# Pinning the order of three engines in the recurrent stage of a hybrid decoder layer

## The chip, the cores and the metric

The kernel runs on one core of one Trainium2 chip. The metric is the device time of one execution in microseconds (us). Of the engines, TensorE (PE; its weight loads are PEld), VectorE (DVE), ScalarE (ACT) and GpSimd (POOL) compute, and SyncE (SP) issues most DMAs. Each takes its instructions in the order in which they stand in its own program; semaphores tie the engines to each other.

## The reference

One decoder layer, batch 1, 1024 tokens, width 1024, all in float32. After an RMSNorm one input projection makes the columns of two branches; both branches are gated by a SiLU, joined, projected out, added to x and normed again.

```
p = rms_norm(x) @ w_in                      # 1024 x 8320
p_tm = p_tm + (prev_token(p_tm) - p_tm) * mu_shift
# RWKV-7, 16 heads of 64, one step per token:
sa    = state @ (-kk)
state = state * decay + sa (kk*a)^T + v k^T
y     = state @ r       # then group norm, + bonus (r.k.r_k) v, * silu(gate)
# 16 heads of attention over three dilated windows, * silu(gate)
out = rms_norm(x + concat(y_rwkv, y_att) @ w_out)
```

## The kernel before

Every big product is made exact enough by splitting each operand into a high and a low float32r part: three matmuls of 128x128 by 128x512 for each 128 rows of the sum, so 24 matmuls for one half-job, that is 128 columns of the projection for 512 tokens (`proj_steps`, L174).

The recurrent stage (`rwkv`, from L284) works on 16 units: eight pairs of heads by two halves of the sequence. A unit's 512 tokens are eight chunks of 64. Its work is a pipeline over four turns of one loop over p: in the turn of unit p, unit p+2 is prepared (`prepare`, `products`: decays, their running sums and exponentials, norms, the products inside a chunk), unit p+1 is turned and its triangular systems are inverted (`late`, `invert`), unit p runs the recurrence (`chain`), and unit p-1 is normed, gated and stored (`finish`).

A turn is cut into 24 slots, three for each chunk. `chain` gives one piece for each slot: first (L707's helper `spread` copies z to zd), second (ud), third (Sd, the new state). Each piece is a small matmul, then a copy of one half on VectorE (L704, L707) and, after it, of the other half on ScalarE (L705, L708), whose result the next piece's matmul reads. The other steps are lists of (slot, function); the loop appends them to the slot's list `ev[s]` and calls them in that order: chain, finish, late, invert, prepare and products. After each slot `advance(4)` issues four matmuls of the projection stream.

The stream (`stream`, L182) works through the projection's columns. At the start of a job, `wload` (L161) issues the two DMAs for the next job's weights, their casts on ScalarE (L170) and their remainders (L171; on VectorE for this stage's columns). After the 24th matmul of a half-job the bank is emptied at once (`take`): for most columns the token shift, L213 on ScalarE and L216 on VectorE. Two PSUM banks serve the stream; one bank (tag `tr`) serves the transposes, the bonus and the inversion in turn, and two (pa0, pa1) serve the decay, the products and the turning of the output.

The program is written with a scheduling layer that sees all instructions. What stands above is only the order of emission: within the data's dependences the layer chooses the order of each engine itself, from emission order as priority and an estimated time for each instruction. It also places all semaphores, and it lets only one engine at a time work on a PSUM bank.

After this stage, attention runs with the rest of the projection stream between its own matmuls, and then the output projection.

Of the kernel before, what the change touches and what calls it, by code (L numbers as in the profile page):

```python
# [19 lines left out]
KT = DM // 128  # L20
# [10 lines left out]
NSLOT = 3 * NC_  # L31
AHEAD = 120
OFILL = 8
WARM = (1, 0)
V_AT = (-2, 3, -1)
COLS = (2, 2, 2, 4, 5, 6, 6, 6, 7, 8, 8, 8, 9, 9, 10)
DECAY = float(np.exp(-0.5))
# [8 lines left out]
class Kern:  # L46
# [114 lines left out]
    def wload(self, src, wp, eng):  # L161

        nc = self.nc
        wl = wp.tile([128, KT, 128], F32R, name="wl")
        wh = wp.tile([128, KT, 128], F32R, name="wh")
        for i in range(2):
            raw = wp.tile([128, KT // 2, 128], F32, name="wraw")
            ks = slice(4 * i, 4 * i + 4)
            nc.sync.dma_start(out=raw, in_=src[i * 512:(i + 1) * 512].rearrange("(kt p) c -> p kt c", p=128))
            nc.scalar.copy(out=wh[:, ks], in_=raw)  # L170
            eng.tensor_tensor(out=wl[:, ks], in0=raw, in1=wh[:, ks].bitcast(F32), op=ALU.subtract)  # L171
        return wh, wl

    def proj_steps(self, w, h, q):  # L174
        wh, wl = w
# [6 lines left out]
    def stream(self, jobs):  # L182

        load = lambda job: self.wload(self.t["w_in"][:, job[0]:job[0] + 128], self.wp,
                                      self.nc.vector if job[0] < ATT0 else self.nc.gpsimd)
        w = load(jobs[0])
        for i, (_, halves, take) in enumerate(jobs):
            wn = load(jobs[i + 1]) if i + 1 < len(jobs) else None
            for h in halves:
                q = self.ps_proj.tile([128, HALF], F32, name="pq", tag="proj")  # L190
                steps = self.proj_steps(w, h, q)
                for m in steps[:-1]:
                    m()
                    yield
                steps[-1]()
                take(h, q)
                yield
            w = wn

    def advance(self, n):  # L200
# [83 lines left out]
    def rwkv(self, pairs=range(NPAIR), apairs=range(NPAIR)):  # L284
        nc = self.nc
        with ExitStack() as ctx:
# [37 lines left out]
            units = [dict(h=h, pr=pr) for pr in pairs for h in range(2)]  # L324
            for i, d in enumerate(units):
                d["AR"], d["Vd"] = self.ARs[i % 3], self.Vds[i % 2]
            N = len(units)
            self.flow = self.stream(self.jobs(units, apairs))
            next(self.flow)
            self.taken = 1  # L330
# [4 lines left out]
            self.lora_w(units[0])  # L335
            for p in range(-2, N):
# [3 lines left out]
                if dC:  # L340
                    put(enumerate(self.chain(dC, get(p + 1) if dC["h"] == 0 else None)))
                if dF:
                    put(self.finish(dF))
                if dI:
                    put(self.late(dI))
                    put(self.invert(dI, self.Us[(p + 1) % 2]))
                if dA:
                    lag = WARM[p + 2] if p < 0 else 0
                    put([(n + lag, f) for n, f in self.prepare(dA) + self.products(dA)])
                if get(p + 3) and get(p + 3)["h"] == 0:  # L350
                    ev[12].append(lambda d=get(p + 3): self.lora_w(d))
                elif get(p + 3):
                    get(p + 3)["lw"] = get(p + 2)["lw"]
                if p == -2:
                    px = self.prep_x(1, self.lng, tags, ba)
                    for s in range(4):
                        ev[s].append(lambda: [next(px, None) for _ in range(2)])
                    ev[4].append(lambda: [None for _ in px])
                n = 5 if p < 0 else 2 if dA is not None and get(p + 3) is None else 4
                for s in range(NSLOT):  # L360
                    for f in ev[s]:
                        f()
                    self.advance(n)
            for _, f in self.finish(units[-1]):
                f()

# [3 lines left out]
    def lora_w(self, d):  # L370

        nc = self.nc
        pc = slice(d["pr"] * 128, d["pr"] * 128 + 128)
        raw = self.mid.tile([128, 128], F32, name="lraw", bufs=1)
        nc.sync.dma_start(out=raw[0:64], in_=self.t["w_up"][:, pc])
        nc.sync.dma_start(out=raw[64:128], in_=self.t["a_up"][:, pc])
        hi = [self.mid.tile([128, 128], F32R, name=f"lhi{i}", bufs=1) for i in range(2)]
        lo = self.llo
        for i in range(2):
            a, b = slice(64 * i, 64 * i + 64), slice(64 - 64 * i, 128 - 64 * i)  # L380
            nc.scalar.copy(out=hi[i][a], in_=raw[a])
            nc.scalar.copy(out=hi[i][b], in_=raw[a])
            nc.gpsimd.tensor_tensor(out=lo[i][a], in0=raw[a], in1=hi[i][a].bitcast(F32), op=ALU.subtract)
        d["lw"] = hi, lo

    def prepare(self, d):

        nc = self.nc
        V, S, G = nc.vector, nc.scalar, nc.gpsimd
        h, pr = d["h"], d["pr"]  # L390
# [48 lines left out]
        t = {}  # L439
# [13 lines left out]
        def norm():  # L453
            sqt = t["q"]
            nq = self.mid.tile([128, 4, 2], F32, name="nq")
            V.tensor_reduce(out=nq, in_=sqt, axis=AX.X, op=ALU.add)
            rn = d["rn"] = self.mid.tile([128, NC_], F32, name="rn", bufs=3)
            for par in range(2):
                for e in range(2):
                    V.tensor_scalar(out=rn[e * 64:e * 64 + 64, par::2], in0=nq[par * 64:par * 64 + 64, :, e], scalar1=1e-24,  # L460
                                    scalar2=-2.0, op0=ALU.max, op1=ALU.mult)
            V.reciprocal(out=rn, in_=rn)
            d["rn1"] = self.mid.tile([64, NC_], F32, name="rn1", bufs=3)
            S.copy(out=d["rn1"], in_=rn[64:128])

        def removal():
            ks, ta, W, Ux = d["ks"], d["ta"], d["W"], d["Ux"]
# [17 lines left out]
        def bonus_parts():  # L485
            rs = d["rs"]
            V.scalar_tensor_tensor(out=rs, in0=rs, scalar=self.hrk[:, pr:pr + 1], in1=d["ks"], op0=ALU.mult, op1=ALU.mult)
            bh, bl = d["bs"] = [self.tmp(t, n, dt=F32R) for t, n in (("kr3", "bh"), ("vr3", "bl"))]
            S.copy(out=bh, in_=rs)
            G.tensor_tensor(out=bl, in0=rs, in1=bh.bitcast(F32), op=ALU.subtract)  # L490
        return [(2, square), (4, squares), (5, norm), (7, decay), (8, rates), (9, logs), (10, lambda: sums(0)), (11, lambda: sums(1)),
                (11, growth), (12, decrease), (13, removal), (14, removal2), (15, removal3), (16, receptance), (21, bonus_parts)]

    def late(self, d):

# [94 lines left out]
    def invert(self, d, U):  # L590

        nc = self.nc
        V, S, G = nc.vector, nc.scalar, nc.gpsimd
# [3 lines left out]
        rs = lambda g: slice(32 * g, 32 * g + 32)  # L597
        t = {}
# [57 lines left out]
        lo = [slice(e * 64, e * 64 + 32) for e in range(2)]  # L656
        hi = [slice(e * 64 + 32, e * 64 + 64) for e in range(2)]
# [19 lines left out]
        def m4c():  # L677
# [122 lines left out]
    def attention(self, ctx, pairs=range(NPAIR), filler=None):  # L800
# [44 lines left out]
        for j, (pr, e) in enumerate(heads):  # L845
# [6 lines left out]
            for i, (qb, n) in enumerate(tiles):  # L852
# [311 lines left out]
```

## Time and profile before

| what | value |
|---|---|
| time, median of 3 runs | 1554.56 us (1554.13 to 1555.15) |
| the profiled execution | 1555.3 us, its span 1553.6 us |
| TensorE busy | 1486.1 us, 96% of the span |
| VectorE busy | 1009.3 us, 65% |
| ScalarE busy | 897.6 us, 58% |
| GpSimd busy | 442.0 us, 28% |
| recurrent units | from about 114 us to 843 us of the span |

Busy time of an engine is the union of its instructions' spans. Matmuls overlap in the pipeline, so a matmul that lasts 0.4 us may start 0.23 us after the one before it; TensorE's busy share says little about how close it is to its limit. The granted clock is given as a share of the full 2.4 GHz.

### The profile page before, as it was taken

What the parts mean: (1) busy time and instruction counts of PE and PEld (TensorE: products, weight loads), DVE (VectorE), ACT (ScalarE), POOL (GpSimd) and SP (SyncE); (2) the same over time, 40 slices, a digit from 0 to 9 for tenths busy, and PEclk for the clock granted to TensorE, in tenths of its full rate; (3) what the DMA queues carried; (4) which work ended last, traced back from release to release, by engine and by line L of the source; (5) the groups of instructions that cost most, each with busy time, mean ns of one, the idle gap of its engine ahead of it and who ended that gap; (6) DMA issues with size and microseconds to landing.
All of it is one profiled execution on the core that took longest, in us unless ns stands there. A gap on an engine that the chain in (4) does not pass through costs nothing.

```text
span 1553.6 us, 29135 instructions
## 1 busy us (share of the span) xinstructions
PE 1486.1 (96%) x10721; PEld 1201.3 (77%) x10721; DVE 1009.3 (65%) x2776; ACT 897.6 (58%) x2080; POOL 442.0 (28%) x563
## 2 busy tenths in 40 slices
PE   5999999999999999999999999999999999899997
PEld 4877777777777777777777788888888888787886
DVE  6866776667776677766743557667676666956144
ACT  6655666666676666666643556555565565655221
POOL 3211111111111121112211534334443343456442
PEclk9999999999999999999999999999999999999999
DMA  6321111111111111111111201111111111426452
GB/s 199 90 48 33 41 40 39 41 34 40 47 32 41 47 33 41 39 38 41 34 39 34 70 28 42 35 35 34 38 52 34 36 55 55 159 92 203 142 161 99
DMA packets 178829, 94.87 MB, mean 61 GB/s; under 512 B 58413, under 2 KB 164606, under 8 KB 178686
## 3 DMA queue, kind: packets, MB, share of 16 engines
q1 hardware_dynamic: 174942, 86.19, 19.4%
q10 hardware_dynamic: 3744, 6.82, 1.3%
q8 instruction: 84, 1.38, 0.4%
q14 instruction: 59, 0.48, 0.1%
HBM read 75.01 MB, written 17.83 MB: 60 GB/s over the span
## 4 chain that ended last, share of the span: by engine, by line
PE 60%; DVE 17%; ACT 16%; issue 3%; DMA 2%; POOL 1%; SPq 0%; DVEq 0%; ACTq 0%; POOLq 0%
PE pq L179 28%; PE oq L1048 10%; PE o L994 3%; PE z L693 3%; PE T L693 3%; PE mp L921 2%; PE sp L954 2%; ACT Y L745 1%; DVE I L422 1%; ACT MV L569 1%; PE sp L974 1%; ACT Vd L513 1%; DVE TB L604 1%; ACT shtmp L213 1%; PE pa L559 1%
## 5 line engine op out<-in xcount | busy, mean ns | idle before, releaser
L179 PE MATMUL pq<-xh,wh 128*128 128x512 f32 x1040 | 429.1, 413 | 0.0
L179 PE MATMUL pq<-xl,wh 128*128 128x512 f32 x1040 | 412.3, 396 | 0.0
L179 PE MATMUL pq<-xh,wl 128*128 128x512 f32 x1040 | 303.3, 409 | 0.0
L179 PEld LDWEIGHTS pq<-xh,wh 128*128 128x128 f32 x1040 | 195.9, 188 | 32.6 <-ACT xh L157 0.3
L179 PEld LDWEIGHTS pq<-xl,wh 128*128 128x128 f32 x1040 | 196.4, 189 | 30.9 <-DVE xl L158 0.4
L179 PEld LDWEIGHTS pq<-xh,wl 128*128 128x128 f32 x1040 | 184.5, 189 | 31.9
L1048 PE MATMUL oq<-ow,qr 128*128 128x512 f32 x512 | 161.9, 394 | 1.2 <-ACT ow L1029 0.6
L982 POOL TENSOR_TENSOR pl<-p,ph 128x512 fp32r<-128x512 f32 (+2 forms) x96 | 102.3, 1072 | 202.2 <-ACT ph L981 182.4
L923 DVE CUSTOM_DVE_ANT_0 mp<-mp,maskq 128x512 f32<-128x512 f32 (+1 forms) x192 | 105.5, 570 | 68.4 <-PE mp L921 59.9
L977 ACT ACTIVATE p<-p 128x512 f32<-128x512 f32 (+2 forms) x144 | 64.6, 452 | 104.2 <-DVE p L976 103.3
L171 POOL TENSOR_TENSOR wl<-wraw,wh 128x512 fp32r<-128x512 f32 x64 | 85.5, 1354 | 110.4 <-PE pq L179 58.4
L1043 POOL TENSOR_TENSOR vr<-kr,qr 128x512 fp32r<-128x512 f32 (+2 forms) x68 | 90.8, 1340 | 80.5 <-ACT qr L1042 70.0
L1048 PEld LDWEIGHTS oq<-ow,qr 128*128 128x128 f32 x512 | 95.9, 188 | 22.8 <-ACT ow L1029 1.1
L1048 PE MATMUL oq<-ow,vr 128*128 128x512 f32 x256 | 101.2, 395 | 1.9 <-POOL vr L1043 1.9
L170 ACT CAST wh<-wraw 128x512 fp32r<-128x512 f32 x138 | 80.7, 616 | 28.6 <-PE pq L179 23.4
L1042 ACT CAST qr<-kr 128x512 fp32r<-128x512 f32 (+2 forms) x68 | 40.2, 594 | 93.5 <-PE oq L1048 52.0
L976 DVE TENSOR_TENSOR p<-sp,maskt 128x512 f32<-128x512 f32 (+2 forms) x144 | 65.2, 457 | 43.3 <-PE sp L974 41.9
L570 POOL TENSOR_SCALAR_AFFINE_SELECT MV<-MV 64x512 f32<-64x512 f32 x64 | 47.8, 747 | 125.2 <-ACT MV L569 114.2
L708 ACT ACTIVATE ud<-z,rn 64x64 f32<-64x64 f32 x128 | 39.3, 307 | 65.3 <-DVE ud L707 63.6
L707 DVE TENSOR_SCALAR ud<-z,rn 64x64 f32<-64x64 f32 x128 | 34.3, 268 | 58.1 <-PE z L693 57.9
L693 PEld LDWEIGHTS T<-ud,TU 128*128 128x128 f32 x256 | 42.5, 188 | 34.8 <-ACT ud L708 28.2
L708 ACT ACTIVATE Sd<-T,dec 64x64 f32<-64x64 f32 x120 | 36.9, 307 | 53.5 <-DVE Sd L707 52.0
(236 smaller groups left out, 3158.4 us busy)
## 6 DMA issues: line engine op xcount, KB each, us to landing
wraw<-in_w_in_dram SPq DMA_DIRECT2D x138, 256.0 KB
kr<-mixd SPq DMA_DIRECT2D x60, 256.0 KB
oraw<-in_w_out_dram SPq DMA_DIRECT2D x16, 512.0 KB
xt<-in_x_dram SPq DMA_DIRECT2D x8, 512.0 KB
ld<-TU SPq DMA_DIRECT2D x32, 128.0 KB
mixd<-zt SPq DMA_DIRECT2D x16, 256.0 KB
mixd<-gt SPq DMA_DIRECT2D x16, 256.0 KB
xr<-in_x_dram ACTq DMA_DIRECT2D x16, 256.0 KB
```

The lines of the kernel that those rows point to most:

```text
L170: nc.scalar.copy(out=wh[:, ks], in_=raw)
L171: eng.tensor_tensor(out=wl[:, ks], in0=raw, in1=wh[:, ks].bitcast(F32), op=ALU.subtract)
L179: return [lambda i=i, a=a, b=b: self.nc.tensor.matmul(q, lhsT=a, rhs=b, start=(i == 0), stop=(i == len(ops) - 1)) for i, (a, b) in enumera ...
L570: G.affine_select(out=f, in_=f, pattern=[[0, 4], [-1, 2], [1, 64]], compare_op=ALU.is_ge, fill=0.0, base=0, channel_multiplier=-1)
L693: mm = lambda out, w, x, start, stop: nc.tensor.matmul(out, lhsT=w, rhs=f2(x), start=start, stop=stop, skip_group_check=True)
L708: S.activation(out=out[er[1], 1], in_=q[0:64, 64:128], func=AF.Copy, scale=scale[1])
L923: V.tensor_tensor_reduce(out=mp[:, :kn], in0=mp[:, :kn], in1=self.maskq[:, v0:v0 + kn], op0=ALU.add, op1=ALU.max, scale=1.0, scalar=-3e38, ...
L976: V.tensor_tensor(out=p[:, :qn], in0=sp[:, :qn], in1=self.maskt[:, u0:u0 + qn], op=ALU.add)
L977: S.activation(out=p[:, :qn], in_=p[:, :qn], func=AF.Exp)
L982: G.tensor_tensor(out=pl[:, :qn], in0=p[:, :qn], in1=ph[:, :qn].bitcast(F32), op=ALU.subtract)
L1043: nc.gpsimd.tensor_tensor(out=ml, in0=raw, in1=mh.bitcast(F32), op=ALU.subtract)
L1048: nc.tensor.matmul(q, lhsT=m[:, i], rhs=v, start=(k == 0 and j == 0), stop=(k == 15 and j == 2))
```

## The change

The turns p = 0 to 15 stand inside a region that pins TensorE, VectorE and ScalarE to the order of emission; SyncE and GpSimd are still ordered by the layer, and so are the two warm-up turns (p = -2, -1). With it, five things about the order of emission change. In a slot the recurrence's piece comes first, then any bank waiting to be emptied, then half of the slot's matmuls, then the other steps, then the other half. `take` is put on a list and called in the slot after the bank's last matmul. `wload` is cut in three: both fetches before the first matmul of a job, the first cast and remainder before its tenth, the second before its sixteenth. `lora_w` is cut in two: the fetch in slot 6, the casts in slot 12. In `prepare` the copy of the norm goes from slot 5 to 6, `decrease` from 12 to 13, `removal` to `removal3` from 13, 14, 15 to 14, 15, 16, the bonus product from 21 to 20 with its split left in 21; in `invert`, m4 goes from 22 to 23.

```diff
+SPLIT_AT = (0, 9, 15)
 def wload(self, src, wp, eng):
-        for i in range(2):
-            raw = wp.tile([128, KT // 2, 128], F32, name="wraw")
-            nc.sync.dma_start(out=raw, in_=src[...])
-            nc.scalar.copy(out=wh[:, ks], in_=raw)
-            eng.tensor_tensor(out=wl[:, ks], in0=raw, in1=wh[:, ks].bitcast(F32), op=ALU.subtract)
-        return wh, wl
+        def fetch():
+            for i in range(2):
+                raws.append(wp.tile([128, KT // 2, 128], F32, name="wraw"))
+                nc.sync.dma_start(out=raws[i], in_=src[...])
+        def split(i):
+            nc.scalar.copy(out=w[0][:, ks], in_=raws[i])
+            eng.tensor_tensor(out=w[1][:, ks], in0=raws[i], in1=w[0][:, ks].bitcast(F32), op=ALU.subtract)
+        return w, [fetch, lambda: split(0), lambda: split(1)]
 def stream(self, jobs):
-                for m in steps[:-1]:
+                for m in steps:
+                    if t in SPLIT_AT and todo:
+                        todo.pop(0)()
+                    t += 1
                     m()
+                    if m is steps[-1]:
+                        if self.pend is None:
+                            take(h, q)
+                        else:
+                            self.pend.append(lambda take=take, h=h, q=q: take(h, q))
                     yield
-                steps[-1]()
-                take(h, q)
-                yield
 def rwkv(...):
                 for s in range(NSLOT):
+                    chain[s]()
+                    if self.pend is not None:
+                        while self.pend:
+                            self.pend.pop(0)()
+                        self.advance(n // 2)
                     for f in ev[s]:
                         f()
-                    self.advance(n)
+                    self.advance(n if self.pend is None else n - n // 2)
+            for p in (-2, -1):
+                unit(p)
+            self.pend = []
+            with self.tc.manual_schedule(engines={mybir.EngineType.PE, mybir.EngineType.DVE, mybir.EngineType.Activation}):
+                for p in range(N):
+                    unit(p)
+            for f in self.pend:
+                f()
+            self.pend = None
 def prepare(...):
-        return [(2, square), (4, squares), (5, norm), (7, decay), (8, rates), (9, logs), (10, lambda: sums(0)), (11, lambda: sums(1)),
-                (11, growth), (12, decrease), (13, removal), (14, removal2), (15, removal3), (16, receptance), (21, bonus_parts)]
+        return [(2, square), (4, squares), (5, norm), (6, norm1), (7, decay), (8, rates), (9, logs), (10, lambda: sums(0)),
+                (11, lambda: sums(1)), (12, growth), (13, decrease), (14, removal), (15, removal2), (16, removal3),
+                (16, receptance), (20, bonus_parts), (21, bonus_split)]
 def invert(...):
-            (22, m4), (23, m4c)]
+            (23, m4), (23, m4c)]
```

## Rows read from the trace of the kernel before

**Rows 1.** Windows of two units: length, busy us (instructions) by engine, clock, DMA.
```profile
395.18:442.33 47.15, 45.27 (x444) 35.46 (x443) 33.14 (x109) 29.92 (x77) 7.43 (x16) 1.00 0.16 40
442.33:489.79 47.46, 45.84 (x444) 35.59 (x443) 33.50 (x109) 31.60 (x83) 8.12 (x16) 1.00 0.15 40
```

**Rows 2.** Timeline of TensorE: start us, us, line, operation, names, shapes, count.
```profile
477.46 0.38 PE L693 MATMUL z<-Sd,AR 128*66 128x128 f32 x2
477.68 0.39 PE L693 MATMUL T<-Vd,MV 128*128 128x128 f32 x2
...
480.18 1.16 PE L559 MATMUL pa<-AR,BK 64*128 64x128 f32 x16
481.27 0.50 PE L179 MATMUL pq<-xh,wh 128*128 128x512 f32 x1
481.61 0.40 PE L179 MATMUL pq<-xl,wh 128*128 128x512 f32 x1
481.84 0.39 PE L179 MATMUL pq<-xh,wh 128*128 128x512 f32 x1
...
484.81 0.69 PE L663 MATMUL x<-UT,TU 32*32 32x32 f32 x32
```

**Rows 3.** Timeline of all engines where the recurrence runs with little beside it.
```profile
838.61 0.42 PE L693 MATMUL T<-ud,TU 128*128 128x128 f32 x2
...
839.07 0.28 DVE L707 TENSOR_SCALAR Sd<-T,dec 64x64 f32<-64x64 f32 x1 [0.92 <-PE T L693]
...
839.38 0.31 ACT L708 ACTIVATE Sd<-T,dec 64x64 f32<-64x64 f32 x1 [0.89 <-DVE Sd L707]
...
840.02 0.38 PE L693 MATMUL z<-Sd,AR 128*66 128x128 f32 x2
...
840.44 0.22 DVE L704 COPY zd<-z 64x64 f32<-64x64 f32 x1 [1.09 <-PE z L693]
...
840.69 0.20 ACT L705 COPY zd<-z 64x64 f32<-64x64 f32 x1 [1.00 <-DVE zd L704]
```

**Rows 4.** Timeline of all engines in a full unit.
```profile
506.51 0.43 PE L693 MATMUL z<-Sd,AR 128*66 128x128 f32 x2
...
507.30 0.21 DVE L704 COPY zd<-z 64x64 f32<-64x64 f32 x1
...
507.74 0.75 DVE L469 SCALAR_TENSOR_TENSOR AR<-ks,prm,W 128x512 f32<-128x512 f32 x1
...
508.41 0.18 DVE L604 TENSOR_TENSOR TB<-UB,AB 64x39 f32<-64x39 f32 x1
```

**Rows 5.** Groups by line, 395 to 490 us: busy us, mean ns, idle before, releaser.
```profile
L539 DVE TENSOR_TENSOR bv<-bq,vs 128x512 f32<-128x512 f32 x2 | 1.3, 672 | 0.0
L469 DVE SCALAR_TENSOR_TENSOR AR<-ks,prm,W 128x512 f32<-128x512 f32 x2 | 1.5, 754 | 0.2
...
L213 ACT ACTIVATE shtmp<-pq,prm 128x512 f32<-128x512 f32 x7 | 4.8, 688 | 0.6 <-PE pq L179 0.3
L170 ACT CAST wh<-wraw 128x512 fp32r<-128x512 f32 x8 | 4.7, 613 | 0.6 <-PE pq L179 0.6
L569 ACT COPY MV<-pa 64x512 f32<-64x512 f32 x8 | 4.7, 582 | 0.9 <-DVE TU L566 0.6
...
L786 ACT COPY zt<-yq 64x256 f32<-64x256 f32 x8 | 2.9, 366 | 0.4 <-PE yq L778 0.3
...
L438 ACT ACTIVATE a<-ta,hk 128x512 f32<-128x512 f32 x2 | 1.6, 816 | 0.0
```

**Rows 6.** Timeline of SyncE, the DMA issues of the inversion's way through memory.
```profile
436.73 1.26 SPq L578 DMA_DIRECT2D ld<-TU  x2
439.87 1.78 SPq L584 DMA_DIRECT2D AB<-ld  x4
```

**Rows 7.** Windows in the attention stage, columns as in rows 1.
```profile
890.00:895.00 5.00, 4.26 (x18) 3.23 (x17) 2.33 (x5) 2.84 (x7) 3.38 (x3) 1.00 0.00 0
895.00:900.00 5.00, 5.00 (x20) 4.12 (x19) 2.97 (x7) 1.73 (x3) 0.00 (x0) 0.66 0.01 2
```

More of the change, by code (lines that the diff above doesn't have):

```diff
@@ L163, in wload @@
         nc = self.nc
-        wl = wp.tile([128, KT, 128], F32R, name="wl")
-        wh = wp.tile([128, KT, 128], F32R, name="wh")
-        for i in range(2):
-            raw = wp.tile([128, KT // 2, 128], F32, name="wraw")
+        w, raws = [], []
+        def fetch():
+            for i in range(2):
+                raws.append(wp.tile([128, KT // 2, 128], F32, name="wraw"))
+                nc.sync.dma_start(out=raws[i], in_=src[i * 512:(i + 1) * 512].rearrange("(kt p) c -> p kt c", p=128))
+        def split(i):
+            if i == 0:
+                w.extend(wp.tile([128, KT, 128], F32R, name=n) for n in ("wh", "wl"))
             ks = slice(4 * i, 4 * i + 4)
-            nc.sync.dma_start(out=raw, in_=src[i * 512:(i + 1) * 512].rearrange("(kt p) c -> p kt c", p=128))
-            nc.scalar.copy(out=wh[:, ks], in_=raw)
-            eng.tensor_tensor(out=wl[:, ks], in0=raw, in1=wh[:, ks].bitcast(F32), op=ALU.subtract)
-        return wh, wl
+            nc.scalar.copy(out=w[0][:, ks], in_=raws[i])
+            eng.tensor_tensor(out=w[1][:, ks], in0=raws[i], in1=w[0][:, ks].bitcast(F32), op=ALU.subtract)
+        return w, [fetch, lambda: split(0), lambda: split(1)]
     def proj_steps(self, w, h, q):
@@ L185, in stream @@
                                       self.nc.vector if job[0] < ATT0 else self.nc.gpsimd)
-        w = load(jobs[0])
+        w, steps = load(jobs[0])
+        for f in steps:
+            f()
         for i, (_, halves, take) in enumerate(jobs):
-            wn = load(jobs[i + 1]) if i + 1 < len(jobs) else None
+            wn, todo = load(jobs[i + 1]) if i + 1 < len(jobs) else (None, [])
+            t = 0
             for h in halves:
@@ L334, in rwkv, with unit @@
             get = lambda n: units[n] if 0 <= n < N else None
-            self.lora_w(units[0])
-            for p in range(-2, N):
+            self.lora_w(units[0])()
+            def unit(p):
                 dA, dI, dC, dF = get(p + 2), get(p + 1), get(p), get(p - 1)
@@ L339, in rwkv @@
                 put = lambda steps: [ev[s].append(f) for s, f in steps]
-                if dC:
-                    put(enumerate(self.chain(dC, get(p + 1) if dC["h"] == 0 else None)))
+                chain = self.chain(dC, get(p + 1) if dC["h"] == 0 else None) if dC else [lambda: None] * NSLOT
                 if dF:
@@ L350, in rwkv @@
                 if get(p + 3) and get(p + 3)["h"] == 0:
-                    ev[12].append(lambda d=get(p + 3): self.lora_w(d))
+                    d = get(p + 3)
+                    ev[6].append(lambda: d.update(split=self.lora_w(d)))
+                    ev[12].append(lambda: d.pop("split")())
                 elif get(p + 3):
@@ L360, in rwkv @@
                 for s in range(NSLOT):
+                    chain[s]()
[3 more added lines that the diff above has]
+                        self.advance(n // 2)
                     for f in ev[s]:
                         f()
-                    self.advance(n)
+                    self.advance(n if self.pend is None else n - n // 2)
[6 more added lines that the diff above has]
+            for f in self.pend:
+                f()
+            self.pend = None
             for _, f in self.finish(units[-1]):
@@ L376, in lora_w, with split @@
         nc.sync.dma_start(out=raw[64:128], in_=self.t["a_up"][:, pc])
[L377 to L384, printed above, removed]
+        def split():
+            hi = [self.mid.tile([128, 128], F32R, name=f"lhi{i}", bufs=1) for i in range(2)]
+            lo = self.llo
+            for i in range(2):
+                a, b = slice(64 * i, 64 * i + 64), slice(64 - 64 * i, 128 - 64 * i)
+                nc.scalar.copy(out=hi[i][a], in_=raw[a])
+                nc.scalar.copy(out=hi[i][b], in_=raw[a])
+                nc.gpsimd.tensor_tensor(out=lo[i][a], in0=raw[a], in1=hi[i][a].bitcast(F32), op=ALU.subtract)
+            d["lw"] = hi, lo
+        return split
     def prepare(self, d):
@@ L462, in norm, with norm1 @@
             V.reciprocal(out=rn, in_=rn)
+        def norm1():
             d["rn1"] = self.mid.tile([64, NC_], F32, name="rn1", bufs=3)
-            S.copy(out=d["rn1"], in_=rn[64:128])
+            S.copy(out=d["rn1"], in_=d["rn"][64:128])
         def removal():
@@ L487, in bonus_parts, with bonus_split @@
             V.scalar_tensor_tensor(out=rs, in0=rs, scalar=self.hrk[:, pr:pr + 1], in1=d["ks"], op0=ALU.mult, op1=ALU.mult)
+        def bonus_split():
+            rs = d["rs"]
             bh, bl = d["bs"] = [self.tmp(t, n, dt=F32R) for t, n in (("kr3", "bh"), ("vr3", "bl"))]
```

## The prediction

> **What bounds the kernel now.** I read the page's 40 slices first: TensorE is busy in 9 tenths of nearly every slice, at the full clock. That looks like a TensorE limit, but a busy share counts a matmul's whole latency, so the second view was the stage by windows, over two whole units (a unit is one pair of heads and one half of the sequence, 24 slots) [rows 1]. Two units last 47.15 + 47.46 = 94.6 us, 47.3 each; VectorE is busy 33.3 of that and ScalarE 30.8. Then TensorE's timeline, for what a matmul takes from start to start [rows 2]: 0.23 us for a 512-column one (481.61 to 481.84), 0.22 for a pair of the 128-column recurrence (477.46 to 477.68, so 0.11 each), 1.09 for the 16 of a products step (480.18 to 481.27), about 0.65 for each group of the inversion (0.69 busy, less the tail of the last). TensorE's own work in a unit is then 96 projection matmuls x 0.23 = 22.1; recurrence, 8 chunks x 12 x 0.11 = 10.6; products 2 x 1.1 = 2.2; 20 transposes x 0.11 = 2.2; 6 wide ones of decay and bonus x 0.23 = 1.4; four inversion groups, 2.8 with their switching. Sum 41.3 us. So 47.3 - 41.3 = 6.0 us of a unit are TensorE waiting, small pieces hidden in its busy time. That is all the change can win here, and what it can enlarge. The recurrence alone does not bound: a step is matmul start to VectorE 0.42 us, to ScalarE 0.25 to 0.31, and ScalarE lasts 0.20 to 0.31 [rows 3], some 1.0 us; 24 steps are 24 us.
>
> **What the pinned order does.** Before, all three engines run in an order that the scheduler chose: the copy zd comes 0.79 us after its matmul (506.51 to 507.30), other VectorE work having been put in front [rows 4], against 0.42 where nothing is in front. After, each engine must take: recurrence piece of slot s, the bank's emptying if one is due, two projection matmuls, the slot's other steps, two more projection matmuls. No instruction is added or taken away, so TensorE's 41.3 us stay. New is that TensorE, standing at a matmul whose input VectorE or ScalarE has not made, holds back ready projection matmuls. So I add TensorE's waits by following the new order of each engine: an instruction starts when its engine is free and its input is there. Costs: a 128x512 VectorE instruction lasts 0.67 to 0.75 (the extremes of some twenty such groups; the relayout, 0.93, and the logs, 0.43, stand apart) [rows 5], and the next starts 0.08 earlier than its end (507.74 to 508.41) [rows 4], so 0.60 to 0.67; ScalarE: bank copy 0.69, weight cast 0.61, each of four quarter copies 0.37, masked copy 0.58, the factor a 0.82 [rows 5]. TensorE's own work in a slot is four projections, 0.92, and a piece of 0.66, 0.22 or 0.44 in turn: 1.58, 1.14 or 1.36, plus the slot's extras (four transposes 0.44, the inversion's groups 0.95, 0.60, 0.62 and 0.62).
>
> Slots 2 to 4 (from the matmul of slot 2 to that of slot 5). VectorE comes to the state copy at 0.91, behind slot 1's mean; state copies 0.27 + 0.31 = 1.49; cast 0.61 = 2.1; subtraction 0.6 = 2.7; three columns 0.9 = 3.6; copy 0.14, square sum 0.6, thirteen small steps of the root 1.3, with which ScalarE's four key copies and second cast are done 0.3 later, subtraction 0.6 = 6.55; copies 0.27 + 0.31 = 7.14. TensorE's own work there is 1.80 + 1.58 + 1.58 = 4.96. Wait 2.2.
>
> Slots 6 and 7. zd copies to 1.0 (0.14 late behind slot 5's norm), bank copy 0.7, four turned copies 1.48 = 3.18; only then is the bank free for decay's matmuls in slot 7, which TensorE reaches at 1.58 + 0.22 + 0.46 = 2.26. Wait 0.9.
>
> Slots 12 to 16 (slot 12 to slot 17). Matmul 0.42, copies 0.43, bank copy 0.69 = 1.54; VectorE's shift 0.66, bonus product 0.60, transpose LT 0.63 = 3.43; ud copies 0.58 = 4.01 (slot 14 starts); ScalarE's exponential 0.60, decay copy 0.25, factor 0.74, state copy 0.31 = 5.91 (slot 15); cast 0.61 = 6.5; VectorE's subtraction 0.60 and removal's two 1.28 = 8.41; copies 0.42 = 8.83 (slot 16); meanwhile VectorE's transpose 0.65, removal2's two 1.28, subtraction 0.60 from 8.55 = 11.08, copies 0.58 = 11.66. TensorE's own: 1.58 + 1.14 + 1.36 + 1.58 + 2.09 = 7.75. Wait 3.9.
>
> Slots 18 and 19. 1.54 as in slot 12; shift 0.66, two masks 1.30, last masked copy 0.6 = 4.1; the products' second step needs both banks, and TensorE is there at 1.58 + 0.60 + 0.22 + 0.46 = 2.86. Wait 1.25.
>
> The rest: slot 11's bonus waits for slot 10's four copies 0.45; slot 22 behind the second masked copies 0.5; slot 0 0.1. Sum: 2.2 + 0.9 + 3.9 + 1.25 + 1.05 = 9.3 us. A unit becomes 41.3 + 9.3 = 50.6, 3.3 more than now. Thirteen units are full: 43 us. The last three lack part of the work and keep perhaps the half to two thirds of the waits' growth, 2 to 2.5 each: 7. Sum 50 us on the profiled execution's 1555.3 (span 1553.6): 1605. The runs' median lies 0.7 lower, which I leave inside the rounding.
>
> **Edits costed at nothing.** Bank emptied one step on: the projection has two banks and comes back to one after 24 matmuls, six slots; the 2 us of delay hide there. Fetch and cast apart: the fetch's place is two slots before the cast, but SP is not pinned and the raw tiles are free some eight slots earlier; without that cover the cast would stand up to 1 us in slots 2 and 14. Small weights' cast apart, the norm's copy, decrease, the bonus split and m4 each one slot on: already in the slots above. Relayout's round trip: from its issue to the block reads 3.1 us (436.73 to 439.87) [rows 6], four issues 1.8 and, by the same round trip, some 2 to land, 7 in all, against about 7.6 from slot 22 to the first column in slot 2: hidden, with only half a us to spare; if it fails, up to 1 us a unit.
>
> The waits have two ends. Below: instructions of one slot overlap more than I let them, as the present order lets some of its waits vanish; with 6.8 instead of 9.3, 0.8 us a unit, 13 x 0.8 + 2 = 12 us: 1567. Above: each hand-over 0.04 us dearer on some 25 hand-overs in the paths, 1 us, and the two DMA waits at 1 us together: 5.3 us a unit, 80 us: 1635. I take 9.3, since all its terms are measured durations.
>
> **Where the skill differs.** The granted clock is 1.00 through the stage [rows 1]; it is 0.66 as the mean of 895 to 900 us, after a stretch in which TensorE was busy 4.26 of 5 us [rows 7]. The Trainium skill, "TensorE: Matmul & The Clock Gate", section "HAM oscillation", says that gaps in TensorE's work can throw it back to the half clock. By that rule the pinned order would pay a second time, as in the third rival; here no window of the stage shows it.
>
> **Rivals.** (1) Faster. Putting the recurrence first in every slot shortens its hand-overs from 0.79 to 0.42 [rows 3, 4], and slot after slot stays at TensorE's own work; the heavy slots' VectorE work is made up in the light ones that follow (slots 13, 17, 19, 21 and 23 have hardly any). With 4 us of waits a unit is 45.3: 14 x 2.0 = 28 us less, 1527. It decides at 6.0 us of waits in a unit, where before and after are equal. For it: VectorE and ScalarE work only 33 and 31 of 47 us. Against: a light slot helps only the slots after it; the path of slots 12 to 16 runs through both engines with no free place.
> (2) No effect: the scheduler's order was nearly that of emission, so that pinning it shifts waits only: 1555. Against: [rows 4], where other work stands before zd.
> (3) Clock falls: if in slots 12 to 19 the clock goes once a unit to half for about 3.4 us (the stretch in [rows 7]: 0.34 x 5 us missing, at half the clock), up to 1.7 us are lost a unit: 1605 + 24 = 1629.
>
> **Chances.** Forecast 0.70; clock or DMA on top 0.08; faster 0.16; no effect 0.06. The likeliest case alone reaches from 1567 to 1635. Some way towards the other cases, 1556 to 1636 holds 8 in 10. Within 0.2% (3 us, about what can be told from no change here) I give 0.05, faster 0.16, slower 0.79.
>
> **What would show it.** Right: units of 50 to 51 us, for instance from one ud issue on SP to the next; slots 12 to 16 near 11.7 us, with TensorE's idle rows released by ud, Sd and zd copies of ScalarE; VectorE waiting for bank copies (shtmp) and casts; attention unchanged and only later. Wrong: units of 46 us or less; or a first column that waits for its DMA; or half clock in the stage.

## The result: 1672 us, 7.6% slower, nearly all of it in TensorE's waits

The changed kernel takes 1672.47 us (median of 4 runs, 1669.43 to 1674.44) against 1554.86 us; the ratio is 1.0758, 95% interval 1.0745 to 1.0771. Slower was right, and so were the places of the waits; the size was not: +118 us against the forecast +50, and outside the range.

| us | before | after |
|---|---|---|
| span of the profiled execution | 1553.6 | 1667.7 |
| first recurrence matmul of unit 0 | 113.6 | 114.8 |
| last chunk of unit 15 begins | 840.0 | 954.4 |
| from there to the end | 713.6 | 713.3 |
| a full unit (mean of units 4 to 11) | 47.32 | 54.70 |
| TensorE busy, whole span | 1486.1 | 1486.5 |

So the whole difference lies in the recurrent stage. Thirteen full units are 7.5 us longer each (97.7), units 13 and 14 by 6.4 and 5.9, the part of unit 15 up to its last chunk by 3.3, the start by 1.1. The attention stage only comes later.

Two units after, in one window; the columns are those of [rows 1]:

```profile
441.95:551.34 109.39, 90.79 (x887) 67.06 (x885) 69.89 (x217) 61.04 (x160) 13.15 (x32) 1.00 0.14 34
```

In two units TensorE is busy 90.79 us, as in [rows 1] (45.27 + 45.84 = 91.11). The window is 109.39 instead of 94.61 us long, the clock 1.00 in both: the growth is TensorE standing still, 9.3 us of a unit instead of 1.75. What it stands for, over the same two units (view of waits, TensorE; us in total, times, longest; `z` and `T` are matmuls of the recurrence, `pa` of the products, `zq` of the decay, `sqt` of the norm), after:

```profile
PE T L732 <- ACT ud L747: 6.3, 6, 1.3
PE z L732 <- ACT zd L744: 4.0, 6, 1.2
PE pa L598 <- ACT MV L608: 2.6, 2, 1.3
PE zq L433 <- ACT zt L825: 1.6, 2, 0.8
PE z L732 <- ACT Sd L747: 1.5, 4, 0.4
PE sqt L482 <- ACT MV L567: 1.2, 2, 0.6
```

and before, over the two units of [rows 1]:

```profile
PE T L693 <- ACT ud L708: 1.2, 2, 0.7
PE z L693 <- ACT zd L705: 0.7, 2, 0.5
PE z L693 <- ACT Sd L708: 0.5, 3, 0.2
```

ScalarE's half of a recurrence copy is named as releaser, but it is only the last link: ScalarE itself waited for VectorE's half (over the whole span `ACT ud` idles 119.6 us for `DVE ud`). The page's chain of waits says the same: VectorE's share is 27% (17% before), TensorE's 52% (60%).

**Slots 2 to 4**, the largest loss, in the timeline of all engines after (start us, us, engine, line, operation, names, shapes, count, idle before and releaser). The first line is the matmul of slot 2, the last that of slot 5:

```profile
445.13 0.42 PE L732 MATMUL T<-ud,TU 128*128 128x128 f32 x2
...
446.89 0.62 ACT L176 CAST wh<-wraw 128x512 fp32r<-128x512 f32 x1
...
447.55 0.69 DVE L177 TENSOR_TENSOR wl<-wraw,wh 128x512 fp32r<-128x512 f32 x1 [1.17 <-ACT wh L176]
...
448.15 0.16 DVE L643 TENSOR_TENSOR TB<-UB,AB 64x15 f32<-64x15 f32 x1
...
449.32 0.21 DVE L743 COPY zd<-z 64x64 f32<-64x64 f32 x1
449.45 0.67 DVE L805 TENSOR_REDUCE gs<-ysq 128x8 f32<-128x512 f32 x1
...
450.15 0.17 DVE L60 TENSOR_SCALAR rs_x<-gs 128x8 f32<-128x8 f32 x1
...
450.36 0.17 DVE L61 TENSOR_SCALAR rs_w<-rs_x 128x8 int32<-128x8 int32 x1
...
450.56 0.17 DVE L63 TENSOR_SCALAR gr<-rs_w 128x8 int32<-128x8 int32 x1
450.64 0.16 DVE L65 TENSOR_SCALAR rs_x<-rs_x 128x8 f32<-128x8 f32 x1
...
452.46 0.69 DVE L177 TENSOR_TENSOR wl<-wraw,wh 128x512 fp32r<-128x512 f32 x1
453.07 0.27 DVE L746 TENSOR_SCALAR ud<-z,rn 64x64 f32<-64x64 f32 x1
...
453.37 0.31 ACT L747 ACTIVATE ud<-z,rn 64x64 f32<-64x64 f32 x1 [1.44 <-DVE ud L746]
...
453.73 0.49 PE L732 MATMUL T<-ud,TU 128*128 128x128 f32 x2 [1.27 <-ACT ud L747]
```

445.13 to 453.73 is 8.6 us, where 7.14 was forecast. Look at the starts on VectorE: two instructions of 0.17 us stand 0.20 apart when the second reads what the first wrote (450.36, 450.56), and 0.08 when it does not (450.56, 450.64: L65 does not read what L63 wrote). The root is a chain, so its thirteen instructions take 2.31 us (450.15 to 452.46). Before, the scheduler had laid the columns (steps of the inversion, L604 and L606, two small instructions each) between the root's steps (VectorE's timeline before, one unit, the same columns):

```profile
400.58 0.17 DVE L606 TENSOR_TENSOR UB<-UB,TB 64x15 f32<-64x15 f32 x1
400.67 0.16 DVE L60 TENSOR_SCALAR rs_w<-rs_x 128x8 int32<-128x8 int32 x1
400.78 0.18 DVE L604 TENSOR_TENSOR TB<-UB,AB 64x28 f32<-64x28 f32 x1
400.88 0.15 DVE L62 TENSOR_SCALAR gr<-rs_w 128x8 int32<-128x8 int32 x1
```

Here a start follows every 0.10 us. From such rows I had taken 0.10 for a step of the root; in the pinned order two chains that could fill each other's gaps run one behind the other.

**Slots 12 to 16** took 12.13 us (468.10 to 480.23; forecast 11.66), by the path that was forecast, through both engines:

```profile
470.46 0.68 DVE L578 TENSOR_TENSOR bv<-bq,vs 128x512 f32<-128x512 f32 x1
...
471.06 0.70 DVE L661 STREAM_TRANSPOSE LT<-TU 128x512 f32<-128x512 f32 x1
471.68 0.23 DVE L746 TENSOR_SCALAR ud<-z,rn 64x64 f32<-64x64 f32 x1
471.95 0.31 ACT L747 ACTIVATE ud<-z,rn 64x64 f32<-64x64 f32 x1 [1.74 <-DVE ud L746]
...
472.31 0.49 PE L732 MATMUL T<-ud,TU 128*128 128x128 f32 x2 [1.29 <-ACT ud L747]
472.63 0.38 PE L732 MATMUL z<-Vd,MV 128*66 128x128 f32 x2
```

From VectorE's start to TensorE's is 0.63 us (471.68 to 472.31), where I had 0.58: each hand-over costs 0.03 to 0.05 us from an end to a start (VectorE to ScalarE 471.91 to 471.95, ScalarE to TensorE 472.26 to 472.31); from the bank copy to the shift on VectorE it is 0.10 (469.69 to 469.79). And the first pair of matmuls behind a wait takes 0.32 (to 472.63) instead of the 0.22 of [rows 2]. By such steps the lag behind the forecast grows from 0.05 us at the bank copy to 0.20 at slot 14, 0.35 at slot 15, 0.43 at slot 16 and 0.47 at the end.

### The profile page after: what moved, and what is told of

Same layout as the page of the kernel before. It is cut to its first block, busy times and chain, and to the rows that moved or that the text cites. A ratio compares the mean times of both kernels' runs of the same rounds, so it can differ in the third digit from the quotient of the medians.

```text
span 1667.7 us, 29002 instructions
## 1 busy us (share of the span) xinstructions
PE 1486.5 (89%) x10721; PEld 1176.8 (71%) x10721; DVE 1035.6 (62%) x2776; ACT 894.6 (54%) x2080; POOL 425.7 (26%) x563
## 4 chain that ended last, share of the span: by engine, by line
PE 52%; DVE 27%; ACT 12%; issue 4%; DMA 4%; SPq 1%; POOL 1%; DVEq 0%; ACTq 0%; POOLq 0%
PE pq L185 24%; PE oq L1087 9%; PE o L1033 3%; PE z L732 2%; DVE TU L605 2%; PE pa L598 2%; PE mp L960 2%; PE T L732 2%; DVE UB L645 2%; PE sp L993 2%; ACT shtmp L227 2%; DVE TB L643 1%; DVE wl L177 1%; ACT Vd L552 1%; ACT wh L176 1%
## 5 line engine op out<-in xcount | busy, mean ns | idle before, releaser
L185 PE MATMUL pq<-xh,wh 128*128 128x512 f32 x1040 | 439.9, 423 | 0.0
L185 PE MATMUL pq<-xh,wl 128*128 128x512 f32 x1040 | 315.0, 413 | 0.0
L185 PEld LDWEIGHTS pq<-xh,wl 128*128 128x128 f32 x1040 | 179.8, 190 | 26.5
L747 ACT ACTIVATE ud<-z,rn 64x64 f32<-64x64 f32 x128 | 39.3, 307 | 120.2 <-DVE ud L746 119.6
L732 PE MATMUL T<-ud,TU 128*128 128x128 f32 x256 | 56.9, 304 | 51.8 <-ACT ud L747 51.8
L744 ACT COPY zd<-z 64x64 f32<-64x64 f32 x128 | 26.1, 204 | 123.9 <-DVE zd L743 123.1
L743 DVE COPY zd<-z 64x64 f32<-64x64 f32 x128 | 26.4, 207 | 100.3 <-PE z L732 100.2
```

Of the source, the lines that this page charges most:

```text
L185: return [lambda i=i, a=a, b=b: self.nc.tensor.matmul(q, lhsT=a, rhs=b, start=(i == 0), stop=(i == len(ops) - 1)) for i, (a, b) in enumera ...
L732: mm = lambda out, w, x, start, stop: nc.tensor.matmul(out, lhsT=w, rhs=f2(x), start=start, stop=stop, skip_group_check=True)
```

## Experiments

Theory: the order of emission on the three engines alone costs the time; TensorE's waits are where the prediction had them, and they are longer because dependent VectorE instructions stand back to back and because of hand-overs that I left out. Rivals: one of the edits costed at nothing (the bank emptied later, fetch and cast apart), the DMA of the relayout, or the clock.

**Which part costs.** Each of these changes one line of the changed kernel.

```diff
-            with self.tc.manual_schedule(engines={mybir.EngineType.PE, mybir.EngineType.DVE, mybir.EngineType.Activation}):
+            if True:                                                   # e1_free
+            with self.tc.manual_schedule(engines={mybir.EngineType.PE}):   # e2_pe_only
+            with self.tc.manual_schedule(engines={mybir.EngineType.DVE, mybir.EngineType.Activation}):   # e3_dve_act
+            with self.tc.manual_schedule(engines={mybir.EngineType.DVE}):  # e9_dve_only
+            with self.tc.manual_schedule(engines={mybir.EngineType.Activation}):  # e10_act_only
```

Expected of all three free: 

> The changed kernel with the region that pins the order left out, all else of the change kept (recurrence first in the slot's emission, banks emptied one step on, weights fetched and cast apart, steps moved). Theory (the pinned order costs: TensorE stands 13.4 us a unit at matmuls whose input is late, against 6.0 before): about 1555 us, 1545 to 1575, units of 47 to 48 us. Rival (the moved steps and the split weight load cost it, in whatever order): within 10 us of 1672.

Expected of TensorE alone: 

> Only TensorE pinned to emission order; VectorE and ScalarE ordered by the layer. Theory that the late inputs come from the fixed order of VectorE and ScalarE: most of the loss goes, 1570 to 1610 us. Rival that TensorE's fixed place for four projection matmuls a slot is what costs, whatever the others do: 1650 to 1672 us.

Expected of VectorE and ScalarE: 

> Only VectorE and ScalarE pinned; TensorE ordered by the layer, so projection matmuls may fill its waits. Theory (in slots 12 to 16 and 2 to 4 the path runs through VectorE and ScalarE alone, and the number of projections to place is the same): 1635 to 1672 us, units of 52 to 54.7. Rival (TensorE's fixed place costs): 1555 to 1600 us.

Expected of VectorE alone: 

> VectorE alone held to the order of emission; TensorE and ScalarE ordered by the scheduling layer. With all three free a unit is 47.0 us, with VectorE and ScalarE held 53.6, with TensorE alone held 48.2. Theory (the waits come of VectorE taking its dependent instructions back to back, and of what stands in front of them): VectorE brings at least two thirds of the 97 us that the pair cost, so 1615 to 1650, likeliest 1625, units near 51.5 us. Rival (the two engines' shares are alike, as the two take turns at each hand-over): 1600. Rival (it needs both; an engine left free arranges itself around the one held): within 15 us of 1555.

Expected of ScalarE alone: 

> ScalarE alone held to the order of emission; TensorE and VectorE ordered by the scheduling layer. Theory: the remaining third of the pair's 97 us or less, 1570 to 1590, likeliest 1580, units near 48.7 us. Rival (shares alike): 1600. Rival (both needed): within 15 us of 1555.

| pinned | us | ratio, 95% interval | unit, us |
|---|---|---|---|
| none | 1553.75 | 0.9994, 0.9985 to 1.0004 | 46.96 |
| TensorE | 1574.99 | 1.0133, 1.0118 to 1.0148 | 48.23 |
| ScalarE | 1576.68 | 1.0146, 1.0129 to 1.0163 | 48.75 |
| VectorE | 1634.82 | 1.0513, 1.0498 to 1.0529 | 52.44 |
| VectorE, ScalarE | 1650.96 | 1.0620, 1.0603 to 1.0638 | 53.6 |
| all three | 1672.47 | 1.0758, 1.0745 to 1.0771 | 54.70 |

With nothing pinned the other edits are worth nothing that can be measured: the pinning is the whole cause, and the edits costed at nothing were costed rightly as long as the order is free. VectorE's order alone is the dearest of the three by far. The single excesses (1.3, 1.5 and 5.1%) add to 7.9% where all together cost 7.6%, but they can't be read as shares of the 118 us, because VectorE alone pays for things that the changed kernel does not. From its third unit on, VectorE waits at the first column for the block reads of the relayout (the inversion's way through memory, [rows 6]), 4.0 to 4.4 us in one full unit and 1.1 to 1.6 in the next:

```profile
435.39 0.17 DVE L643 TENSOR_TENSOR TB<-UB,AB 64x15 f32<-64x15 f32 x1 [4.02 <-DMA AB<-ld]
```

In the changed kernel no full unit has such a wait. With VectorE alone held, the clock also falls in six of the thirteen full units (at up to 1.6 us each, the price that e4 below shows), with VectorE and ScalarE held in seven, in the changed kernel in none. How much of VectorE's 80 us is the same waits as in the changed kernel is therefore not shown, and that the sum comes out near is luck.

**Before's own order pinned.** Expected: 

> The kernel before with nothing but the region added: its own emission order pinned on the three engines, without the moved steps, the later emptying of banks and the split weight load. Theory (late inputs behind fixed places; the change's moves were to soften them): slower than the changed kernel, 1690 to 1750 us. Rival (the moves are what makes the pinned order dear): below 1672 us.

```diff
 (the kernel before)
-            for p in range(-2, N):
+            for p in (-2, -1):
+                unit(p)
+            with self.tc.manual_schedule(engines={PE, DVE, Activation}):
+                for p in range(N):
+                    unit(p)
```

1774.19 us, ratio 1.1425 (1.1398 to 1.1452), above the expected range, and 63.15 us a unit. The change's moves therefore win about 100 us of what the pinning alone would cost; they have no such worth in a free order, where the first run above puts them at nothing. Much of the 100 us may be the clock: it is 0.92 and 0.87 over two units of 60.7 and 65.7 us, so 6.7 us of full clock are missing in a unit, of the 8.45 by which a unit is longer than the changed kernel's, and the changed kernel has no fall in a full unit. That is an upper bound, since TensorE also waits there.

**The root's dependent steps.** Two ways: put the three columns of slot 2 between the root's steps (e4), and give the root one Newton step instead of three, six instructions fewer (e6; e7 the same unpinned).

```diff
 e4:  def call(**kw):                 # wraps VectorE inside the root
+         r = f(**kw)
+         if self.weave:
+             self.weave.pop(0)()      # one half of a column
+         return r
 e6, e7:
-        for _ in range(3):
+        for _ in range(its):          # its = 1 for the output's norm
```

Expected of e4: 

> All three pinned, but the three columns of slot 2 (six small VectorE instructions, each needing the one before) are emitted between the thirteen small steps of the group norm's root in slot 3, one after each. Same instructions, only their order. Theory (a small VectorE instruction that reads its predecessor's result starts 0.20 us after it, an independent one 0.07 to 0.11, and slots 2 to 4 are on the path): chunk 1 falls from 8.1 to about 6.9 us, 1.1 us a unit, 1655 us. Rival (what was under-sized is a dearer hand-over between engines, not this): no change, 1669 to 1676 us.

Expected of e6: 

> All three pinned; the group norm's root takes one Newton step instead of three (two thirds of the iteration are left out), six small dependent VectorE instructions fewer in slot 3. Theory (each holds the path 0.20 us in the pinned order): chunk 1 falls by 0.9 to 1.2 us, 0.9 us a unit, 1658 us. Rival (each costs its 0.07 to 0.1 us of the free order, or is hidden): 1665 to 1673 us.

Expected of e7: 

> The same root with one Newton step instead of three, in the kernel of the first experiment, where no order is pinned. Theory (there the small steps stand between other VectorE work and hide): 1550 to 1555 us, no more than 3 us below 1553.75. Rival (they are as dear in any order): 1538 to 1543 us.

e4 took 1665.39 us, ratio 1.0719 (1.0703 to 1.0735): 7 us won where 17 were expected. Its VectorE timeline has the steps 0.09 to 0.12 us apart while a column stands between two of them, and 0.20 again once the columns are used up:

```profile
449.27 0.17 DVE L663 TENSOR_TENSOR UB<-UB,TB 64x15 f32<-64x15 f32 x1
449.36 0.16 DVE L55 TENSOR_SCALAR gr<-rs_w 128x8 int32<-128x8 int32 x1
449.47 0.18 DVE L660 TENSOR_TENSOR TB<-UB,AB 64x28 f32<-64x28 f32 x1
...
450.42 0.17 DVE L55 TENSOR_TENSOR rs_w<-gr 128x8 f32<-128x8 f32 x1
450.63 0.17 DVE L55 TENSOR_TENSOR rs_w<-rs_w,rs_x 128x8 f32<-128x8 f32 x1
```

The three slots from slot 3 on (chunk 1) fall from 8.09 to 7.25 us (expected 6.9). But in seven of the thirteen full units the clock falls right after a TensorE wait of 1.3 us. In units 7 and 11 it is the wait for ud in these slots, which then take 8.86 us. In units 0, 2, 4, 8 and 12 it is the wait for the products' banks in slot 19, and slots 18 to 20 take 9.1 to 9.2 us instead of 7.57. The first kind, in windows of 5 us (columns as in [rows 7]; the first two are unit 7, the other two the same places in unit 6, which has no fall):

```profile
500.00:505.00 5.00, 4.18 (x27) 3.11 (x26) 3.69 (x21) 4.83 (x12) 0.00 (x0) 1.00 0.20 57
505.00:510.00 5.00, 3.71 (x15) 2.94 (x14) 4.40 (x18) 0.70 (x3) 0.00 (x0) 0.69 0.18 52
446.00:451.00 5.00, 4.17 (x26) 3.24 (x26) 3.69 (x21) 4.79 (x12) 0.00 (x0) 1.00 0.29 64
451.00:456.00 5.00, 3.69 (x24) 2.92 (x23) 4.33 (x18) 0.95 (x4) 0.00 (x0) 1.00 0.18 52
```

In 505 to 510 it is 1.2 GHz for part of the window and 2.4 for the rest. A fall costs 1.6 us (8.86 against 7.25, 9.16 against 7.57), so a gain of 0.84 us becomes a loss of 0.8 in a unit with a fall; in the profiled execution, the slowest of its four, nearly all is given back (span 1666.5 against 1667.7). Why seven units have a fall and six have none is not shown: units 3, 5 and 9 have the same instructions in the same order as 7 and 11, and the changed kernel stands through waits of 1.3 us at the same places without one.

e6 took 1660.85 us, ratio 1.0685 (1.0664 to 1.0706). Chunk 1 fell by only 0.49 us (expected 0.9 to 1.2), because ScalarE's second cast is the next limit, and VectorE stands 0.6 us for it:

```profile
449.88 0.62 ACT L176 CAST wh<-wraw 128x512 fp32r<-128x512 f32 x1
450.53 0.69 DVE L177 TENSOR_TENSOR wl<-wraw,wh 128x512 fp32r<-128x512 f32 x1 [0.62 <-ACT wh L176]
```

That is the limit that the prediction had put there. That the time still comes near the expected 1658 is not all the root's doing: in the profiled executions (spans 1667.7 and 1657.0) the thirteen full units give 4.3 us and the last three, where the clock falls once instead of four times, 6.9. e7, unpinned, is 1549.3 us, ratio 0.9969 (0.9957 to 0.9980): the same six instructions are worth 4.5 us against e1, a little more than the 3 that were expected at most.

**VectorE's load.** The weights' remainders moved to GpSimd:

```diff
-                                       self.nc.vector if job[0] < ATT0 else self.nc.gpsimd)
+                                       self.nc.gpsimd)
```

Expected: 

> All three pinned; the weight remainders of this stage (four wide VectorE instructions a unit, in slots 2, 3, 14 and 15) are computed on GpSimd instead. Theory (those slots lie on paths that run through VectorE in its fixed order, so each 0.6 to 0.7 us instruction there is late time for TensorE, and a second one behind it waits for ScalarE's cast): a unit falls from 54.7 by 3 to 4.5 us, 1610 to 1630 us. Rival (what is late is the hand-over between engines, not VectorE's own work): by 1 us or less, above 1655.

1670.28 us, ratio 1.0746 (1.0723 to 1.0768): a miss. Half of the units do what was expected (52.4 us; chunk 1 from 8.09 to 6.43, chunk 5 from 8.62 to 7.59), the other half are 54.6 to 56.8 us long. The thirteen full units together win 7.9 us, and the start takes back more: the first recurrence matmul is at 125.2 us instead of 114.8, as the edit reaches the weights before unit 0 too (why it costs so much there was not followed). In the long units the relayout's block reads come late, and now nothing covers them (SyncE's issues, a late and a punctual unit):

```profile
444.94 1.31 SPq L617 DMA_DIRECT2D ld<-TU  x2
449.83 1.81 SPq L623 DMA_DIRECT2D AB<-ld  x4
...
501.00 1.26 SPq L617 DMA_DIRECT2D ld<-TU  x2
504.13 1.81 SPq L623 DMA_DIRECT2D AB<-ld  x4
```

and the first column of the late unit, with a step of the root behind it:

```profile
453.19 0.76 DVE L643 TENSOR_TENSOR TB<-UB,AB 64x15 f32<-64x15 f32 x1 [1.76 <-DMA AB<-ld]
...
457.65 1.27 POOL L177 TENSOR_TENSOR wl<-wraw,wh 128x512 fp32r<-128x512 f32 x1 [3.72 <-ACT wh L176]
457.82 1.12 DVE L71 TENSOR_TENSOR rs_w<-rs_w,rs_x 128x8 f32<-128x8 f32 x1
```

4.9 us from one issue to the other instead of 3.1, then a wait of 1.76 us, and behind it the clock falls again (chunk 1 10.3 us). The moved work itself also stands in the way: the root's step takes 1.12 us instead of 0.17 and ends 0.02 us after the GpSimd remainder that began just before it. The five other long units have the same, and the first column's 0.76 us ends with a remainder too; that the one holds up the other is read from these ends alone. The delay is in the changed kernel too (439.88 to 444.45, 4.6 us, in one unit; 494.83 to 497.97 in the next), only the column is not ready before 448.15 there. From the block reads' issue to a column that waits for them are 3.36 us (449.83 to 453.19), so 444.45 + 3.36 = 447.81: the changed kernel has 0.34 us to spare. In both late windows, and in neither punctual one, the instruction queue moves one packet beside the relayout's. So it is over all thirteen full turns of the changed kernel: six relayouts take 4.3 to 4.6 us, with instruction packets beside each, and seven take 3.1, with none. That this is the cause was not tested.

**ScalarE's half of the recurrence.** Both halves of each copy on VectorE, which takes the hand-over to ScalarE out of every step:

```diff
-                S.copy(out=out[er[1], 1], in_=q[0:64, 64:128])
+                V.tensor_copy(out=out[er[1], 1], in_=q[0:64, 64:128])
-                S.activation(out=out[er[1], 1], in_=q[0:64, 64:128], func=AF.Copy, scale=scale[1])
+                V.tensor_scalar(out=out[er[1], 1], in0=q[0:64, 64:128], scalar1=scale[1], scalar2=None, op0=ALU.mult)
```

Expected of e11, pinned: 

> All three engines held, but both halves of each of the recurrence's 24 copies on VectorE instead of the second half on ScalarE. Per slot this takes away the hand-over from VectorE to ScalarE (0.034 us) and makes the second half an instruction of VectorE (0.14 to 0.21 us more of it) in place of ScalarE's 0.20 to 0.31; ScalarE gains some 6 us a unit and VectorE pays 4 to 5. Theory (hand-overs and ScalarE's place in the chain are among the terms I left out): a unit falls from 54.7 by about 3 us, so 1625 to 1645. Rival (VectorE sets nearly every wait, and its added 4 to 5 us come on top in the slots where it is late): unit as now or longer, 1665 to 1700.

Expected of e12, unpinned: 

> As the run before it, but with all three engines ordered by the scheduling layer. Theory (a free order hides the hand-overs only in part: a shorter recurrence step leaves fewer holes in TensorE): 3 to 12 us below the kernel before, 1543 to 1552. Rival (a free order already hides them, and VectorE's added work comes to the fore): 1553 to 1565.

e11 took 1643.41 us, ratio 1.0573 (1.0557 to 1.0588): 29 us won, as the theory had it; a full unit is 52.86 instead of 54.70, 1.8 us less where about 3 were expected. VectorE's timeline shows where:

```profile
438.88 0.27 DVE L746 TENSOR_SCALAR ud<-z,rn 64x64 f32<-64x64 f32 x1
439.16 0.28 DVE L747 TENSOR_SCALAR ud<-z,rn 64x64 f32<-64x64 f32 x1
...
439.49 0.49 PE L732 MATMUL T<-ud,TU 128*128 128x128 f32 x2 [2.42 <-DVE ud L747]
```

0.61 us from the first half to the matmul, hardly less than 0.63 to 0.66 before. What helps instead is, as far as these rows go, ScalarE free of 24 instructions a unit (not tested by itself): chunk 5 (8.62) is 8.20 and 8.49, chunk 3 (5.74) 5.45, chunk 4 (6.26 and 6.04) 4.98 and 4.78. So the gain came, but less by the hand-over than I thought. Chunk 1 is worse, 10.04 and 9.85 us, with TensorE waiting 2.42 us and the clock fallen (0.91 and 0.87 over 432 to 448.5).

e12 took 1546.65 us, ratio 0.9950 (0.9935 to 0.9965): faster than both kernels, 8 us below before, as expected. Its units alternate between 45.7 and 47.4 us:

```profile
392.87:438.59 45.72, 44.39 (x445) 33.86 (x443) 39.68 (x132) 23.34 (x54) 7.36 (x16) 1.00 0.16 40
438.59:486.00 47.41, 45.08 (x445) 34.48 (x444) 39.78 (x134) 25.11 (x60) 7.42 (x16) 1.00 0.16 40
```

VectorE is busy 39.7 us of a unit, 6 more than in [rows 1], and it costs nothing: with a free order the load of VectorE is not what counts.

## Why the prediction was wrong

**What holds.** The bound: TensorE with 41.3 us of own work and its waits. No instruction is added, and TensorE's busy time is the same. The places: every wait that was forecast is there, and none where none was forecast is larger than 0.6 us. VectorE does wait for casts (1.17 us at 447.55), attention is only later, and the scheduler's order before was far from that of emission (rival 2 falls; e1 and e8). Rival 1, slots staying at TensorE's own work, falls with 13.4 us of waits a unit, where 6.0 decide. Rival 3 is not what made the changed kernel slow: two units show 1.00, and no full unit of the profiled execution has a fall; only the last three units do (the tail, below).

**The step that failed: the size of the waits.** The sum had 9.3 us a unit; measured are 54.7 - 41.3 = 13.4. The 4.1 us, with the slots compared one by one in the unit at 441.95 (which is 54.9 long, so 4.3 there; a forecast is the own work of the slots and the waits that the sum had in them):

| stretch | forecast | measured | excess |
|---|---|---|---|
| slots 2 to 4 | 7.14 | 8.60 | 1.46 |
| slot 7 | 2.98 | 3.21 | 0.23 |
| slot 8 | 1.36 | 1.92 | 0.56 |
| slot 11 | 2.26 | 2.50 | 0.24 |
| slots 12 to 16 | 11.66 | 12.13 | 0.47 |
| slots 17 to 19 | 8.23 | 8.96 | 0.73 |
| all others | 17.0 | 17.6 | 0.6 |

In slots 2 to 4 the root is 1.0 us longer than its 1.3, 0.3 of which the cast would have covered anyway; the three columns take 1.17 instead of 0.9, the square sum 0.70 instead of 0.60 because the root reads it, and 0.4 goes to hand-overs and to ScalarE (0.26 of it before the cast: VectorE's half of Sd is done at 446.38, but ScalarE is at a quarter copy until 446.54). The forecast's sentence "all its terms are measured durations" was true and misled: the durations were measured in an order that keeps dependent instructions apart, and the spacing that I took from [rows 4], the next start 0.08 us before the end, holds for independent neighbours. In the pinned order the two become neighbours.

The other excesses are 0.05 to 0.3 in nearly every slot: hand-overs of 0.03 to 0.05 us, 0.10 behind a bank copy, and the slow first pair behind a wait. In slot 8 it is VectorE's own queue: the state copy starts at 461.70 for a matmul of 460.45, behind a gate and two dependent column steps, which the forecast had at nothing. From slot 18 to the products' second step are 4.53 us (482.99 to 487.52) where 4.1 was forecast. And [rows 3] itself has 0.46 us from matmul to VectorE for Sd (838.61 to 839.07), where I gave 0.42 for every step. I had named the hand-overs as the upper bound, 0.04 us on 25 of them, and then left them out of the value and put the bound itself too low: the upper end had 5.3 us a unit, the growth was 7.4.

**The tail.** For the last three units I took half to two thirds of the growth, 7 us; measured are 6.4, 5.9 and 3.3, 15.6 in all. They lack preparation, not the recurrence and the root: in units 14 and 15 the three slots from slot 3 on take 8.99 and 9.16 us instead of 3.67 and 4.86. About 1 us of each is a small step of the root that ends together with a GpSimd remainder (882.60, 1.12 us long, and 925.27, 1.30 us), as in e5. Here the third rival has a part too: from 840.9, 854.5, 885.2 and 929.6 us on TensorE runs at half the clock for a while, which the kernel before does nowhere in these units, as in this window:

```profile
840.00:845.00 5.00, 4.71 (x19) 3.72 (x20) 4.54 (x14) 2.84 (x7) 1.42 (x1) 0.66 0.12 30
```

At the 1.6 us that such a fall cost in e4, the four would be up to 6 of the 15.6 us; how much they did cost was not tried.

**The edits costed at nothing** are so in a free order (ratio 0.9994). The list left out one move, `growth` from slot 11 to 12; its ScalarE instruction (469.58 to 470.21) is done before the ud copy at 471.95 and cost nothing. The relayout has 0.34 us to spare in its late units, near the half of a us that I had, but by luck: the way takes 7.9 us (439.88 to 447.81) instead of 7, and the room is 8.3 (to 448.15) instead of 7.6. e5 shows that this is a real bound: whatever makes slots 0 to 2 shorter by more than that gets the difference back as a DMA wait.

**The clock.** In the changed kernel's steady units no window shows it. In e3, e4, e5, e8, e9 and e11 full units have falls; in e4 each came right after a wait of TensorE of 1.3 us and took back 1.6 us (8.86 against 7.25). The Trainium skill, "TensorE: Matmul & The Clock Gate", section "HAM oscillation", tells of gaps that throw TensorE back to the half clock; e4's windows agree as to direction (0.69 behind the wait). By that rule a pinned order that is made shorter but keeps its gaps can still lose. In e4's profiled execution the falls are where the win of slots 2 to 4 went.

## What to carry to other kernels

When an order is to be pinned, follow each engine's new neighbours: an instruction that reads the one before it starts after its end (0.20 us apart for 0.17 us), an independent one before it (0.08 to 0.12), so count chains at the first figure and interleave two of them by hand. Put every hand-over between engines into the sum, not into its bound, and look for what a shorter stretch will meet next: a cast, a DMA with 0.3 us to spare, a GpSimd instruction beside VectorE's, or the clock. Pin nothing that the layer orders well: here the free order with the recurrence's copies on one engine was the best of all kernels tried.

## What was not expected of the hardware

- VectorE: small instructions of 0.17 us, 0.20 us apart when dependent and 0.08 to 0.12 when not (rows of slots 2 to 4, and of e4).
- The first two matmuls of 128 columns behind a wait take 0.32 us instead of 0.22 (472.31 to 472.63).
- A transfer of the same size and shape, 3.1 us from its issue to the next step's issue in one unit and 4.6 to 4.9 in the other, in a steady turn (SyncE's rows in the changed kernel and in e5).
- A VectorE instruction of 0.17 us took 1.12 beside a GpSimd remainder and ended with it (e5, 457.82).
- The clock fell after waits of 1.3 us in seven of e4's thirteen full units, once after a stretch where TensorE was busy 4.18 of 5 us; units with the same instructions and waits had no fall.
